# A new order of work and loads for the opening of a pooling and state-space decoder step, and a new order for the low parts of the pooled rows

## The chip, the cores and the metric

The kernel runs on one core of one Trainium2 chip. The metric is the device time of one execution in microseconds (us), lower is better. The core has a matrix engine (TensorE, PE in the profile), a vector engine (VectorE, DVE), a scalar engine (ScalarE, ACT), a general engine (GpSimd, POOL) and a sync engine (SP) that here only issues DMAs. Each engine runs its own queue of instructions strictly in order and waits for the others at semaphores.

## The reference

One layer of a hybrid decoder is computed for a prompt of 1024 rows and for 64 sample rows (8 sequences of 8), so 1088 rows in all. Cut to what matters:

```python
mod = silu(c) @ w_ada + b_ada
shift, scale, gate = split(mod, 3)
h = rmsnorm(x, norm_g) * (1 + scale) + shift
u_pool, z_pool, z_ssm, xbc, dt_raw, g_raw = split(h @ w_in, SPLITS)
p, pool_new = pool_mix(u_pool, pool_buf, pos0, pool_w, pool_scale)
p = (p * silu(z_pool)) @ w_pool_out
xbc_c, conv_new = causal_conv(xbc, conv_buf, conv_w, conv_b)
y, ssm_new = ssd(xs, dt, A, Bm, Cm, ssm_state)
s = rmsnorm((y + d_skip * xs) * silu(z_ssm), ssm_norm_g) @ w_ssm_out
m = sigmoid(g_pool) * p + sigmoid(g_ssm) * s
x = x + gate * (m @ w_o)
```

The width of the model is 1024, `w_in` has 8224 columns, and the pooling branch has four groups of 128 columns.

## The kernel before

**Stages.** First comes the opening (`first`): the rows of x are loaded, normalised and transposed, the modulation is multiplied out, and the first columns of `h @ w_in` are made. Then come the remaining columns of `h @ w_in` in pairs, by a Strassen scheme of 14 short products per pair (`strassen`, lines L412, L421, L426 and L434 in the profile). After them the chunks of the state-space scan run beside the products with `w_pool_out` and `w_ssm_out` (L227). The product with `w_o` ends the program.

**Two parts for every number.** Products run on a rounded type. So an operand is cut into a high part (a copy by ACT) and a low part (a subtraction, on DVE or POOL), and each product is made of three: high by high, low by high, high by low.

**The opening's order.** `ORDER1` is a list of some 350 words, written out by hand. Each word calls a small function that issues one or a few instructions; each engine then runs its own in that order (`in_line`). A letter at the end of a word sets the engine: V for DVE, A for ACT, G for POOL. The rows are treated in three blocks, 0 (rows 0 to 255), 1 (to 639) and 2 (to 1087); the 1024 columns in eight groups k of 128. The words that matter:

- `sq`, `root`, `unit`, `spread`, `rsb`: the norm of each row and its spreading over the partitions. `turn b.k` transposes a block on PE, `out b.k` takes it out of PSUM on DVE (L703, into a tile `tf`).
- `ada p.k`, `mr p`, `end p`, `md p`: part p (0 to 3) of the modulation, on PE, ACT, PE and DVE (L751, L754). Part p serves the columns k = 2p and 2p + 1.
- `h b.k` makes the high part of the modulated rows (ACT), `t` and `ta` the modulated rows themselves (L776 on ACT, L778 on DVE), `l b.k` their low part (a subtraction, L644). `hi`, `lo` cut weights in the same way, `wh`, `wl` those of the first Strassen pair.
- `pr b.k` are plain products of two weight columns (L817), `sg` takes them out through a sigmoid and stores them.
- `ca`, `cb`, `cc`, `ce` with k = 0 to 3 form the sums and differences of row halves in `tf` for the first Strassen pair (L644, 128x544); `s1` to `s4` cut these into high (`s1h`) and low parts (`s1l`). `ce3` is the last of the sums.
- `dR`, `dU`, `dL` are the products for the time steps (L843); they read the finished sums. `gt` are the products for the gate (L870), `ge` adds the gate's bias. `m i.s` are the 14 products of the first Strassen pair (L958), `u i.s` takes them out.
- `warm n` are n products of ones by ones with no use for the result (L726).

**The opening's loads.** They are issued by SP in the order of the list `waiting`; some have to wait for a word. SP has eight DMAs under way at most: each further one waits for the one eight before it. The loads of state rows for the first pooling and convolution units (L526, L528, L1068) are asked for later in the program, and the tile scheduler puts them where it finds room.

**The pooled rows.** `p_split` reads the four pooled groups back, makes their high parts on ACT and their low parts (L1575) on POOL for groups 0 and 2 and on DVE for 1 and 3. It is advanced step by step from `samples_beside`, which runs once after every product (seven a pair) in the last ten pairs; at the 70th call it issued all four low parts behind the last instruction of DVE. The first product of the next stage (L227) reads the low parts in the order 0, 1, 2, 3 as its last four terms.

Of the kernel before, what the change touches and what calls it, by code (L numbers as in the profile page):

```python
# [46 lines left out]
def tile_pool_ssd_step(  # L47
# [475 lines left out]
    def u_unit(gi):
        L = gi + 1
        stp = sm.tile([P, 120], F32, tag="stc", name=nm("stp"), bufs=4)
        load(stp, state_pool[gi])  # L526
# [14 lines left out]
        V.tensor_copy(us[:, :, 0:15], stv)  # L541
# [59 lines left out]
    ORDER1 = """
        warm20 sq0.A silu sq1.V turn0.3 turn0.5 turn0.2 tab vt sq2.V turn0.6 turn0.1 root0
        turn0.4 warm4 unit0.V sq3.A spread0 sq4.A warm2 rsb0.V out0.4 turn1.2 root1 turn1.5 warm5
        unit1.V out0.2 sq6.A out0.6 spread1 out0.3 out0.5 turn1.7 out0.1 rsb1.A turn1.3 sq7.V sq5.A turn1.6
        turn1.0 turn0.0 warm2 out1.5 sq8.A out1.2 turn2.5 out1.7 turn2.2 root2 out0.0 turn2.4 unit2.A out1.6
        turn2.7 out1.3 turn2.0 out1.0 turn2.1 spread2 ada0.0 rsb2.A ada0.2 out2.2 ada0.4 out2.7 ada0.6
        out2.1 mr0 turn2.3 out2.4 hi0.0 end0 out2.3 turn0.7 hi1.0 lo0.0.G turn1.4 md0 turn2.6 out0.7 turn1.1
        h1.0 out2.6 ada1.0 h0.0 lo1.0.V warm4 t0.0.A out1.4 h0.1 out2.0 ada1.2 t0.1.A l0.0.V warm1 ta2.0.A
        pr0.0 l0.1.V out2.5 t1.0.A pr0.1 t2.0 ta2.1.A out1.1 ada1.4 h2.0 l1.0.V ada1.6 h1.1 t2.1 l2.0.V
        pr1.0 mr1 h2.1 t1.1.A l2.1.G pr2.0 l1.1.V end1 pr2.1 md1 ta2.3.V h1.2 pr1.1 h0.3 t1.2.V t0.3.A t2.3  # L610
        ada2.0 l1.2.V h0.2 ada2.2 h2.3 t0.2.V ada2.4 hi0.1 l0.3.V l2.3.V ada2.6 h1.3 l0.2.V hi1.1 pr1.2
        t1.3.V mr2 lo1.1.V ta2.2.A end2 l1.3.G pr0.2 md2 pr0.3 t2.2 ta2.4.A lo0.1.V pr1.3 h1.4 t2.4 h0.5
        t1.4.V h2.2 ada3.0 t0.5.V h2.4 ada3.2 l2.2.V h1.5 ada3.4 l2.4.G h0.4 ada3.6 t1.5.A l0.5.V pr2.2 mr3
        dwd ta2.5.A l1.5.V t0.4.V end3 t2.5 pr2.3 l0.4.V h2.5 l1.4.G md3 pr0.4 h0.7 l2.5.V wh0 pr0.5 t0.7.V
        h0.6 wl0.V pr1.4 h1.6 tc.V h1.7 ca1.V m0.0 t0.6.A ca0.V s1h1 cb0.V s1h0 pr1.5 u0.0 cc0.V wh1 m0.1
        ce0.V ta2.7.A l0.6.V s4h0 wl1.V t1.6.A pr0.6 l0.7.V tb.V u0.1 pr2.4 wh4 d21.V t1.7.A l1.6.V pr0.7
        ta2.6.A wl4.V pr1.6 l1.7.V sgt t2.6 t2.7 m1.0 cb1.V sg0.0 cc1.V sg0.1 pr1.7 ce1.V h2.7 s1l0.V h2.6
        pr2.5 sg1.1 l2.7.V sg1.0 m1.1 l2.6.V d12.V s4h1 ca2.V pr2.6 wh5 cb2.V s1h2 ca3.V pr2.7 s1l2.V
        s1h3 cb3.V cc2.V gt0 wh3 u1.0 sg2.0 wl3.G u1.1 dR0 wh2 gt2 sg2.1 ce2.V dR1 cc3.V s2h0 gt4 wl2.V
        s4h2 dU1 ce3.V s2h3 s4l2.V s2h2 dL0 dUo1 s2l3.V dU0 s4h3 s2l0.V z1.0 s2l2.V gt6 dUo0 s1l3.V s2h1 dL1  # L620
        ge s4l1.G s3h0 dLo0 m2.0 s3h1 dLo1 s3h3 s3l1.V s3h2 s2l1.V m2.1 u2.0 dsL s3l3.V z1.1 s3l2.V m3.0
        s3l0.V wh6 u2.1 dRo1 wl6.G dRo0 m3.1 dsR u3.0 s4l3.V s1l1.V m4.0 nw u3.1 wl5.V m4.1 u4.0 s4l0.V m5.0
        n1 u4.1 nt3 m5.1 u5.0 nt2 z5.0 m6.0 u5.1 n2 m6.1 u6.0 z5.1 nd u6.1
    """.split()

    def first():
# [195 lines left out]
        def sg(b, t):  # L822
            o, n = BLK[b]
            if b < 2:
                buf = pa.tile([P, HF], F32, tag=("u3", "u2", "c2", "u3")[2 * b + t], name=nm("g0"))
# [4 lines left out]
            act(buf[:, :n], give(("pr", b, t))[:, :n], AF.Sigmoid)  # L830
# [169 lines left out]

        def bg_load():
            for j in range(4):
                load(bg[32 * j:32 * j + NB + 1], b_ada[0, 2 * D + 256 * j:2 * D + 256 * j + 256].partition_broadcast(NB + 1))
# [559 lines left out]
    def p_split():  # L1563
        ph, pl = Y4(hs), Y4(hs)
        ph_.extend(ph[:, gi] for gi in range(4))
        pl_.extend(pl[:, gi] for gi in range(4))
        for gi in range(4):
            load(pl[:, gi].bitcast(F32), yp_d[:, gi])
        yield
        for gi in range(4):  # L1570
            act(ph[:, gi], pl[:, gi].bitcast(F32), AF.Copy)
        yield
        for gi in range(4):
            y = pl[:, gi].bitcast(F32)
            (nc.gpsimd if gi % 2 == 0 else V).tensor_tensor(pl[:, gi], y, ph[:, gi].bitcast(F32), ALU.subtract)  # L1575
# [714 lines left out]
```

## Time and profile before

| | us |
|---|---|
| median of 3 runs | 1208.33 (1208.1 to 1209.11) |
| the profiled execution | 1206.63 |
| its span, first to last instruction | 1204.9 |
| DVE busy in the span | 915.8 |
| ACT busy | 661.4 |
| POOL busy | 815.0 |

In a row of a timeline the numbers are the start from the span's beginning and the time taken, both in us, then the engine, the line of the kernel, the operation, what it writes and reads, and the count. Square brackets give idle time of that engine just before, and who ended it. Neighbouring instructions on one engine overlap by some 0.05 to 0.1 us in these rows, since the next one starts while the last one is written out.

### The profile page before, as it was taken

How to read it: one execution, taken by the hardware profiler on the slowest of the kernel's cores; microseconds unless marked ns; L12 is line 12 of the kernel's file. 1: busy time of each engine (PE TensorE's matmuls, PEld its weight loads, DVE VectorE, ACT ScalarE, POOL GpSimd, SP SyncE). 2: the span in 40 equal slices, each digit the busy share in tenths (PEclk: the TensorE clock that was granted, in tenths of full speed). 3: DMA queues.
4: the chain of work that ended last, by engine and by line, in shares of the span. 5: the costliest groups of instructions: out<-in, count | busy, mean ns of one | idle time of the engine just before them, and what ended most of it. 6: DMA issues, size and time to landing. Idle time of an engine off the chain costs nothing.

```text
span 1204.9 us, 25116 instructions
## 1 busy us (share of the span) xinstructions
PE 1190.0 (99%) x9274; PEld 1125.3 (93%) x9274; DVE 915.8 (76%) x1567; ACT 661.4 (55%) x1511; POOL 815.0 (68%) x687
## 2 busy tenths in 40 slices
PE   9999999999999999999999999999999999999997
PEld 8879999999999999999999999999999989999885
DVE  6993689975979587877576564687888988679976
ACT  6864356475665556554534334566686766412435
POOL 1127878877988787755677776376889889523653
PEclk9999999999999999999999999999999999999999
DMA  9836445565546555454576767988788788595794
GB/s 352 305 133 208 141 137 180 185 212 149 185 157 201 172 160 164 149 166 137 191 241 239 239 220 252 322 311 267 238 273 297 263 293 282 204 337 157 236 208 158
DMA packets 156082, 262.69 MB, mean 218 GB/s; under 512 B 31280, under 2 KB 79160, under 8 KB 155960
## 3 DMA queue, kind: packets, MB, share of 16 engines
q1 hardware_dynamic: 87208, 171.25, 42.7%
q10 hardware_dynamic: 64592, 81.91, 19.7%
q0 software_dynamic: 4160, 7.94, 3.1%
q8 instruction: 73, 1.20, 0.4%
q14 instruction: 49, 0.40, 0.1%
HBM read 173.31 MB, written 87.73 MB: 217 GB/s over the span
## 4 chain that ended last, share of the span: by engine, by line
PE 82%; DVE 5%; DMA 4%; POOL 3%; ACT 3%; issue 2%; SPq 0%; DVEq 0%; POOLq 0%; ACTq 0%
PE mm L412 24%; PE ps L412 24%; PE mm L227 15%; PE pc L412 5%; PE ps L1246 2%; PE ps L1249 2%; DMA Y<-in_w_ada 1%; PE ps L2043 1%; PE ps L2042 1%; PE ps L2041 1%; DVE tf L644 1%; PE ps L1513 1%; PE ps L958 1%; PE pc L1335 1%; DMA G<-in_w_ada 1%
## 5 line engine op out<-in xcount | busy, mean ns | idle before, releaser
L227 PE MATMUL mm<-Y,w 128*128 128x352 f32 (+1 forms) x1440 | 255.4, 331 | 0.8 <-DVE G L1976 0.6
L227 PEld LDWEIGHTS mm<-Y,w 128*128 128x128 f32 x1440 | 235.3, 188 | 7.6 <-issue 4.6
L154 POOL TENSOR_TENSOR w<-rawA,w 128x512 fp32r<-128x512 f32 x120 | 181.7, 1518 | 78.6 <-ACT w L151 72.2
L154 POOL TENSOR_TENSOR w<-raw,w 128x512 fp32r<-128x512 f32 x90 | 157.2, 1753 | 62.9 <-ACT w L151 62.7
L412 PE MATMUL mm<-Y,w 128*128 128x272 f32 x1200 | 168.7, 289 | 0.0
L412 PE MATMUL ps<-Y,w 128*128 128x272 f32 x1200 | 167.8, 289 | 0.0
L412 PEld LDWEIGHTS mm<-Y,w 128*128 128x128 f32 x1200 | 156.8, 188 | 2.6 <-issue 1.0
L412 PEld LDWEIGHTS ps<-Y,w 128*128 128x128 f32 x1200 | 157.1, 188 | 0.8 <-issue 0.6
L151 ACT ACTIVATE w<-rawA 128x512 fp32r<-128x512 f32 x120 | 75.2, 626 | 95.1 <-PE ps L412 53.8
L1090 DVE SCALAR_TENSOR_TENSOR GA<-GA,cvT,GA 128x1112 f32<-128x1112 f32 x72 | 126.1, 1756 | 0.1
L151 ACT ACTIVATE w<-raw 128x512 fp32r<-128x512 f32 x90 | 56.0, 628 | 102.7 <-PE ps L412 33.7
L412 PE MATMUL mm<-G,w 128*128 128x272 f32 x720 | 101.2, 289 | 0.0
L412 PE MATMUL ps<-G,w 128*128 128x272 f32 x720 | 100.6, 289 | 0.0
L412 PEld LDWEIGHTS mm<-G,w 128*128 128x128 f32 x720 | 94.1, 188 | 1.2 <-issue 0.9
L412 PEld LDWEIGHTS ps<-G,w 128*128 128x128 f32 x720 | 94.4, 188 | 0.3 <-issue 0.3
L1234 ACT ACTIVATE dec<-dec,acT 128x128 f32<-128x128 f32 x256 | 78.6, 390 | 18.7 <-POOL dec L1230 18.6
L291 POOL TENSOR_TENSOR pw<-pw 128x512 fp32r<-128x512 f32 x40 | 65.6, 1639 | 11.5 <-ACT pw L290 11.5
L412 PE MATMUL pc<-Y,w 128*128 128x272 f32 x480 | 67.2, 288 | 0.0
L412 PEld LDWEIGHTS pc<-Y,w 128*128 128x128 f32 x480 | 62.6, 188 | 0.5 <-issue 0.4
L1470 POOL TENSOR_TENSOR Y<-xb,Y 128x512 fp32r<-128x512 f32 x32 | 41.5, 1296 | 25.0 <-ACT Y L1468 24.8
L1246 PE MATMUL ps<-dec,xd 128*64 128x128 f32 (+1 forms) x576 | 52.3, 273 | 0.6 <-DVE dec L1535 0.5
L1527 POOL TENSOR_TENSOR xl<-xw,xh 128x512 fp32r<-128x512 f32 x32 | 42.5, 1327 | 14.6 <-ACT xh L1526 14.6
(542 smaller groups left out, 2712.0 us busy)
## 6 DMA issues: line engine op xcount, KB each, us to landing
rawA<-in_w_in SPq DMA_DIRECT2D x62, 512.0 KB
ws<-pw ACTq DMA_DIRECT2D x32, 512.0 KB
dec<-acs_d SPq DMA_DIRECT2D x32, 512.0 KB
w<-ws SPq DMA_DIRECT2D x32, 512.0 KB
xbc<-GA ACTq DMA_DIRECT2D x24, 512.0 KB
wo<-ph SPq DMA_DIRECT2D x20, 512.0 KB
Y<-wo SPq DMA_DIRECT2D x10, 1024.0 KB
pw<-in_w_ssm_out ACTq DMA_DIRECT2D x32, 256.0 KB
```

What stands on the lines that cost most here:

```text
L151: ins = act(hi[:, :, :ncols], raw[:, :, :ncols], AF.Copy)
L154: (eng or nc.gpsimd).tensor_tensor(lo[:, :, :ncols], raw[:, :, :ncols], hi[:, :, :ncols].bitcast(F32), ALU.subtract)
L227: mm(ps[:, :n], w[k // 4][h][:, k % 4, :], r[k][:, o:o + n], start=(j == 0), stop=(j == len(terms) - 1))
L291: nc.gpsimd.tensor_tensor(raw.bitcast(F32R), raw, hi.bitcast(F32), ALU.subtract)
L412: mm(p, w[j // 8][:, k], A(k, s)[j // 4 == 1], start=(j == 0), stop=(j == 11))
L644: eng[e].tensor_tensor(dst, x, y, op)
L1090: V.scalar_tensor_tensor(d[:, :n], rp[:, k:k + n], cvT[:, 24 * k + mc:24 * k + mc + 1], d[:, :n], ALU.mult, ALU.add)
L1234: act(dec[:, h], dec[:, h], AF.Exp, bias=acT[:, c, 8 * g + h:8 * g + h + 1], scale=-1.0)
L1246: mm(o[hh], xd[:S, 2 * q + hh, :], dec[:S, 2 * q + hh], start=True, stop=state is None)
L1249: mm(o[hh], state[:, h * 64:h * 64 + 64], cE[:, h], start=False, stop=True)
L1470: nc.gpsimd.tensor_tensor(yl[g][:, :, o:o + S], v, yhc.bitcast(F32), ALU.subtract)
L1527: nc.gpsimd.tensor_tensor(xl, xw, xh.bitcast(F32), ALU.subtract)
```

## The change

The change has four parts: a new list `ORDER1`; a new order in `waiting`; the state loads of the first units put behind the load of the gate's bias; a new order of the low parts in `p_split`, now in two steps. One tag of a tile in `sg` changes too. Of `ORDER1` only the first line is shown; the diff below is cut to the rest.

```diff
     yp_ = [None] * 4
+    calm = []
...
-        load(stp, state_pool[gi])
         pwt = sm.tile([P, P], F32, tag="stc", name=nm("pwt"), bufs=4)
-        load(pwt, pool_w[0, gi])
+        with tc.issue_after(calm[0]):
+            load(stp, state_pool[gi])
+            load(pwt, pool_w[0, gi])
...
-        warm20 sq0.A silu sq1.V turn0.3 turn0.5 turn0.2 tab vt sq2.V turn0.6 turn0.1 root0
+        warm20 sq0.A silu sq1.V warm5 turn0.0 turn0.2 turn0.3 warm2 sq2.V tab root0 sq3.A sq4.A
...
-                buf = pa.tile([P, HF], F32, tag=("u3", "u2", "c2", "u3")[2 * b + t], name=nm("g0"))
+                buf = pa.tile([P, HF], F32, tag=("u3", "u2", "c2", "g3")[2 * b + t], name=nm("g0"))
...
         def bg_load():
             for j in range(4):
-                load(bg[32 * j:32 * j + NB + 1], b_ada[0, 2 * D + 256 * j:2 * D + 256 * j + 256].partition_broadcast(NB + 1))
+                ins = load(bg[32 * j:32 * j + NB + 1], b_ada[0, 2 * D + 256 * j:2 * D + 256 * j + 256].partition_broadcast(NB + 1))
+            calm.append(ins.ins)
...
-        for what in ("x01", "vb", "x27", "smp", "p0", "w", "p1", "p2"):
+        for what in ("x01", "x24", "vb", "x57", "w0", "smp", "p0", "w1", "p1", "p2"):
...
-            elif what == "w":
-                waiting += [((), lambda t=t: w_load(t, 0)) for t in range(2)]
+            elif what[0] == "w":
+                waiting += [((), lambda t=int(what[1]): w_load(t, 0))]
...
         stc = sm.tile([P, 24], F32, tag="stc", name=nm("stc"), bufs=4)
-        load(stc, state_conv[mc])
+        with tc.issue_after(calm[0]):
+            load(stc, state_conv[mc])
...
-        for gi in range(4):
+        for gi in (0, 2, 1, 3):
             y = pl[:, gi].bitcast(F32)
             (nc.gpsimd if gi % 2 == 0 else V).tensor_tensor(pl[:, gi], y, ph[:, gi].bitcast(F32), ALU.subtract)
-        yield
+            if gi % 2:
+                yield
...
-        if due[0] == 7 * LAST:
+        if due[0] in (7 * LAST - 1, 7 * LAST):
             with behind(mybir.EngineType.DVE):
                 next(p_in)
```

In the new `ORDER1` thirteen words have another engine. From POOL to DVE go `lo0.0`, `l2.1`, `l1.3`, `l2.4`, `l1.4`, `wl3` and `s4l1`; from ACT to DVE `ta2.1` and `t0.3`; from DVE to ACT `unit1`, `t0.2` and `t0.4`; from DVE to POOL `l0.5`. The `warm` words fall from seven to six (38 products to 36). Beyond the opening and the low parts, the engines' sequences stay as they were.

POOL in the opening, before; a name is the tile written, then the tiles read, and the first row is a memset at the program's start:

```order
21 L999 MEMSET bg 128x256
22 L644 TENSOR_TENSOR w_489<-raw_243,w_489 128x512
23 L644 TENSOR_TENSOR Y_520<-tf_310,Y_519 128x448
24 L644 TENSOR_TENSOR Y_520<-tf_290,Y_519 128x384
25 L644 TENSOR_TENSOR G_761<-tf_315,G_760 128x448
26 L644 TENSOR_TENSOR G_761<-tf_315,G_760 128x384
27 L644 TENSOR_TENSOR w_1057<-raw_931,w_1057 128x512
28 L644 TENSOR_TENSOR Y_520<-tf_294,Y_519 128x544
29 L644 TENSOR_TENSOR w_1213<-rawA_715,w_1213 128x512
```

And now (L649 is L644 of before):

```order
21 L1004 MEMSET bg 128x256
22 L649 TENSOR_TENSOR G_747<-tf_363,G_746 128x256
23 L649 TENSOR_TENSOR w_1207<-rawA_709,w_1207 128x512
24 L154 TENSOR_TENSOR w_1249<-rawA_1245,w_1249 128x512
25 L154 TENSOR_TENSOR w_1305<-rawA_1245,w_1305 128x512
```

The seven subtractions `lo0.0`, `l2.1`, `l1.3`, `l2.4`, `l1.4`, `wl3` and `s4l1` have left POOL, and `l0.5` (row 22) has come; the weight of the last product, `wl6`, stays.

SP, whose rows are DMAs, in the middle of the opening, before:

```order
17 L798 DMA raw_263<-in_w_in 128x512
18 L526 DMA stp_1366<-in_state_pool 128x120
19 L528 DMA pwt_1368<-in_pool_w 128x128
20 L1068 DMA stc_1640<-in_state_conv 128x24
21 L1068 DMA stc_1642<-in_state_conv 128x24
22 L798 DMA raw_500<-in_w_in 128x512
23 L197 DMA G_595<-in_w_ada 128x1024
```

And now (L803 is L798 of before):

```order
17 L803 DMA raw_263<-in_w_in 128x512
18 L803 DMA raw_505<-in_w_in 128x512
19 L197 DMA G_594<-in_w_ada 128x1024
20 L197 DMA G_596<-in_w_ada 128x1024
21 L197 DMA G_598<-in_w_ada 128x1024
22 L197 DMA G_600<-in_w_ada 128x1024
23 L509 DMA dtw<-in_w_dt 128x256
```

The four state loads are gone from between the second halves of the plain products' weights; they now stand behind the four loads of the gate's bias.

DVE around the last of the sums (`ce3`, row 122 before, which makes `tf_366`), before:

```order
119 L644 TENSOR_TENSOR tf_306<-tf_306,tf_298 128x544
120 L644 TENSOR_TENSOR tf_290<-tf_366,tf_290 128x544
121 L644 TENSOR_TENSOR w_1071<-rawA_633,w_1071 128x512
122 L644 TENSOR_TENSOR tf_366<-tf_366,tf_290 128x544
123 L644 TENSOR_TENSOR Y_520<-tf_306,Y_519 128x544
124 L644 TENSOR_TENSOR Y_1090<-tf_290,Y_1090 128x544
125 L644 TENSOR_TENSOR Y_1090<-tf_385,Y_1090 128x544
126 L644 TENSOR_TENSOR Y_1090<-tf_298,Y_1090 128x544
```

And now (`ce3` is row 123, L981 is L976 of before):

```order
121 L649 TENSOR_TENSOR tf_303<-tf_358,tf_303 128x544
122 L981 TENSOR_TENSOR c_127_1086<-s_109_895,ps_994 128x272
123 L649 TENSOR_TENSOR tf_358<-tf_358,tf_303 128x544
124 L981 TENSOR_TENSOR c_127_1086<-s_109_895,ps_962 128x272
125 L649 TENSOR_TENSOR Y_1082<-tf_295,Y_1082 128x544
126 L649 TENSOR_TENSOR Y_1082<-tf_303,Y_1082 128x544
127 L649 TENSOR_TENSOR Y_1082<-tf_299,Y_1082 128x544
128 L649 TENSOR_TENSOR w_1063<-rawA_622,w_1063 128x512
129 L649 TENSOR_TENSOR S_1061<-tf_358,S_1061 128x544
130 L649 TENSOR_TENSOR Y_521<-tf_349,Y_520 128x544
131 L649 TENSOR_TENSOR w_1133<-raw_906,w_1133 128x512
```

One `u1` (row 124), the weight `wl2` (row 128) and the weight `wl3` from POOL (row 131) now stand behind `ce3` on DVE.

More of the change, by code (lines that the diff above doesn't have):

```diff
@@ L601, in tile_pool_ssd_step @@
     ORDER1 = """
-        warm20 sq0.A silu sq1.V turn0.3 turn0.5 turn0.2 tab vt sq2.V turn0.6 turn0.1 root0
[L603 to L621, printed above, removed]
@@ L622, in tile_pool_ssd_step @@
-        s3l0.V wh6 u2.1 dRo1 wl6.G dRo0 m3.1 dsR u3.0 s4l3.V s1l1.V m4.0 nw u3.1 wl5.V m4.1 u4.0 s4l0.V m5.0
-        n1 u4.1 nt3 m5.1 u5.0 nt2 z5.0 m6.0 u5.1 n2 m6.1 u6.0 z5.1 nd u6.1
+        warm20 sq0.A silu sq1.V warm5 turn0.0 turn0.2 turn0.3 warm2 sq2.V tab root0 sq3.A sq4.A
+        unit0.V vt spread0 rsb0.V turn0.4 out0.4 root1 turn1.2 out0.2 warm4 unit1.A turn0.1 turn0.6 out0.6
+        spread1 turn1.7 turn1.5 out0.3 sq6.A turn0.5 rsb1.A turn1.3 out1.5 turn1.0 out0.5 sq7.V out1.0 sq5.A
@@ new lines, in tile_pool_ssd_step @@
+        sq8.A out0.1 out1.7 root2 turn2.0 turn1.6 turn0.7 out1.3 unit2.A out0.7 turn1.1 out1.2 turn1.4 turn2.5
+        out1.4 out0.0 spread2 rsb2.A turn2.1 turn2.2 hi0.0 turn2.7 ada0.0 ada0.2 out2.1 ada0.4 out2.5 ada0.6
+        out1.1 warm4 out2.2 mr0 out1.6 end0 turn2.4 lo0.0.V out2.0 md0 turn2.3 hi1.0 out2.7 out2.4
+        h0.0 h0.1 lo1.0.V turn2.6 ada1.0 ada1.2 t0.0.A l0.0.V t0.1.A ta2.0.A pr0.0 h1.0 t2.0 l0.1.V
+        t1.0.A h2.0 warm1 pr0.1 out2.3 t2.1 out2.6 l1.0.V ada1.4 ada1.6 mr1 h1.1 ta2.1.V t1.1.A
@@ new lines, in tile_pool_ssd_step @@
+        l2.0.V pr1.0 l1.1.V h2.1 end1 pr2.0 md1 pr1.1 ta2.3.V l2.1.V pr2.1 ada2.0 h0.3 h1.2
+        ada2.2 h0.2 t0.3.V t2.3 ada2.4 h2.3 t0.2.A t1.2.V l1.2.V l2.3.V ada2.6 h1.3 hi1.1 pr1.2
+        l0.2.V l0.3.V t1.3.V mr2 end2 ta2.2.A lo1.1.V t2.2 pr0.2 md2 hi0.1 ta2.4.A t2.4 h0.5
+        l1.3.V pr0.3 lo0.1.V pr1.3 ada3.0 h1.4 t0.5.V ada3.2 h2.2 h1.5 h2.4 t1.4.V ada3.4 l2.2.V
+        h0.4 ada3.6 pr2.2 mr3 dwd t0.4.A l0.5.G t1.5.A end3 pr2.3 l0.4.V wh0 md3 h0.7
+        ta2.5.A t2.5 l1.4.V h1.7 h2.5 h0.6 l2.4.V h1.6 l1.5.V pr2.4 wl0.V pr0.4 tc.V t0.7.V
@@ L624, in tile_pool_ssd_step @@
+        s2l0.V s2h2 dL0 z1.0 s2h1 s2l3.V s2l2.V dL1 dUo1 wh3 wl2.V dUo0 s1l3.V s4l2.V
+        gt6 s3h0 wl3.V dLo1 s3h3 s4h3 m2.1 s3h1 dLo0 s2l1.V m2.0 s3l0.V s3h2 ge
+        z1.1 s3l1.V u2.0 m3.0 wh6 wl6.G s3l2.V u2.1 s3l3.V m3.1 dRo1 dRo0 u3.1 u3.0
+        s1l1.V m4.0 nw m4.1 dsR s4l1.V wl5.V u4.0 s4l0.V s4l3.V m5.0 nt3 m5.1 dsL
+        u5.0 u4.1 n1 nt2 m6.0 u5.1 n2 u6.0 z5.0 m6.1 z5.1 nd u6.1
     """.split()
```

6 lines of the change are left out of this document (added).

## The prediction

> **What bounds the kernel now.** The page first, then the windows of 25.9 to 72.4 us:
>
> ```profile
> PE 1190.0 (99%) x9274; PEld 1125.3 (93%) x9274; DVE 915.8 (76%) x1567; ACT 661.4 (55%) x1511; POOL 815.0 (68%) x687
> ```
>
> ```profile
> core 0: us, PE busy (x) PEld busy (x) DVE busy (x) ACT busy (x) POOL busy (x), PEclk, DMA share, GB/s
> 25.90:72.40 46.50, 44.39 (x479) 37.33 (x467) 43.49 (x92) 37.83 (x71) 8.17 (x6) 1.00 0.68 256
> ```
>
> PE is busy 99% of the span, so only a stage in which PE waits, or runs below its pace, can give time back. The opening is one: it ends when the first Strassen product behind it starts, and from there PE runs dense for hundreds of us in an unchanged order. So the change is worth what it moves that start. The window shows who paces it: DVE is busy 43.49 of 46.50 us, more than ACT, and PE's timeline names DVE at its last stop:
>
> ```profile
> 72.49 0.87 PE L843 MATMUL ps<-tf,dtw 128*32 128x272 f32 x9 [0.57 <-DVE tf L644]
> ...
> 90.43 1.68 PE L412 MATMUL ps<-Y,w 128*128 128x272 f32 x12
> ```
>
> The time-step products (L843) wait for the sums on DVE; `ce3` frees the last. Behind them stand fourteen products of 1.5 us, four of them done early, and the stage ends at 90.43.
>
> **Part 1: DVE between `md0` and `ce3`.** DVE's and POOL's timelines side by side:
>
> ```profile
> 24.46 1.29 POOL L644 TENSOR_TENSOR w<-raw,w 128x512 fp32r<-128x512 f32 x1 [19.88 <-ACT w L802]
> ...
> 38.94 1.53 POOL L644 TENSOR_TENSOR Y<-tf,Y 128x384 fp32r<-128x384 f32 x1 [5.35 <-PE mm L817]
> 43.44 2.30 POOL L644 TENSOR_TENSOR G<-tf,G 128x448 fp32r<-128x448 f32 x2 [2.97 <-ACT G L769]
> 66.80 1.38 POOL L644 TENSOR_TENSOR w<-raw,w 128x512 fp32r<-128x512 f32 x1 [21.06 <-ACT w L802]
> 68.14 1.84 POOL L644 TENSOR_TENSOR Y<-tf,Y 128x544 fp32r<-128x544 f32 x1
> ```
>
> ```profile
> 25.11 0.67 DVE L754 TENSOR_TENSOR md<-md,vT 128x18 f32<-128x18 f32 x1
> 25.70 0.17 DVE L751 TENSOR_TENSOR md<-ps,vT 128x18 f32<-128x18 f32 x1
> ...
> 34.12 0.18 DVE L754 TENSOR_TENSOR md<-md,vT 128x18 f32<-128x18 f32 x1
> ...
> 39.71 0.80 DVE L754 TENSOR_TENSOR md<-md,vT 128x18 f32<-128x18 f32 x1
> ...
> 43.47 1.40 DVE L644 TENSOR_TENSOR G<-tf,G 128x256 fp32r<-128x256 f32 x1
> 44.79 1.09 DVE L644 TENSOR_TENSOR dwd<-dtw 128x128 f32<-128x128 f32 x1
> ...
> 46.99 0.42 DVE L644 TENSOR_TENSOR G<-tf,G 128x256 fp32r<-128x256 f32 x1
> ...
> 66.96 1.80 DVE L644 TENSOR_TENSOR tf<-tf,tf 128x544 f32<-128x544 f32 x1
> ...
> 69.38 1.82 DVE L644 TENSOR_TENSOR tf<-tf,tf 128x544 f32<-128x544 f32 x2
> ...
> 71.72 0.71 DVE L644 TENSOR_TENSOR tf<-tf,tf 128x544 f32<-128x544 f32 x1
> ```
>
> The same DVE instruction takes 0.18 us alone and 0.67 or 0.80 beside POOL, 0.42 alone and 1.40 beside POOL, 0.71 and 1.80. So a subtraction given to POOL isn't free for DVE. Summed between `md0` (ends 25.87) and `ce3` (ends 72.43): 0.62 at 39.71, 0.98 at 43.47, 0.8 at 44.79 (half of 0.42 as the undisturbed time, its row being half as wide), 1.09 at 66.96 and 0.4 at 69.38 (1.82 less twice 0.71), together **3.9 us**. The order rows show that all six POOL subtractions of this stretch (the window's x6) leave POOL and that only one short one, `l0.5`, comes. A pair as wide cost DVE 1.78 in 2.30 us of POOL; for 256 columns in place of 832 I take 0.6. Contention falls by **3.3 us**.
>
> What does DVE take on? Groups by line and shape in that window:
>
> ```profile
> L644 DVE TENSOR_TENSOR w<-raw,w 128x512 fp32r<-128x512 f32 x4 | 2.7, 684 | 0.0
> ...
> L778 DVE TENSOR_SCALAR tf<-tf,md 128x384 f32<-128x384 f32 x4 | 1.9, 479 | 0.3 <-ACT Y L767 0.3
> ...
> L703 DVE TENSOR_TENSOR tf<-mm,rsb 128x448 f32<-128x448 f32 x3 | 1.8, 610 | 0.0
> ...
> L644 DVE TENSOR_TENSOR G<-tf,G 128x448 fp32r<-128x448 f32 x3 | 1.8, 622 | 0.0
> ...
> L644 DVE TENSOR_TENSOR G<-tf,G 128x384 fp32r<-128x384 f32 x3 | 1.6, 549 | 0.0
> L778 DVE TENSOR_SCALAR tf<-tf,md 128x256 f32<-128x256 f32 x4 | 1.6, 411 | 0.4 <-ACT Y L767 0.3
> ```
>
> New between the two marks: `l2.1` and `l2.4` (0.62 each), `l1.3` and `l1.4` (0.55 each), `ta2.1` and `t0.3` (0.48 each), three `out` of block 2 (0.61 each): 5.13. Gone from it: `t0.2`, `t0.4` and `out0.7` (0.41 each), `l0.5` (0.42), `out1.1` and `out1.4` (taken as `l` of 384, 0.55 each), two `out` of block 2 (1.22), one `u1` (taken as 0.42), `wl2` (0.68): 5.07. That is **no change** in work; what counts is that POOL's part is gone.
>
> Waits: DVE stood idle 46.50 less 43.49, 3.0 us. The longest named:
>
> ```profile
> DVE Y L644 <- ACT tf L776: 1.1, 2, 0.9
> DVE tf L778 <- ACT Y L767: 0.5, 2, 0.3
> DVE R L644 <- ACT R L909: 0.4, 1, 0.4
> ```
>
> ```profile
> ACT g L830 <- DMA gs<-g: 1.0, 1, 1.0
> ```
>
> The last is ACT waiting for a store to free the tile that `sg` uses twice; the new tag takes it away, and ACT feeds DVE. Going through both queues with these durations, ACT mostly has its tile ready now. Nothing in the rows excludes that the waits stay (0) or go (-3.0); I take the middle, **-1.5 us**.
>
> The Trainium skill has a rule for the contention, in SBUF — State Buffer, section "Who interferes with whom": a DVE instruction with two SBUF inputs and a GpSimd instruction that reads SBUF exclude each other for the whole instruction. The trace agrees in kind, though 3.9 us were lost beside 7.05 us of POOL in these rows; by full blocking the sum below would be some 3 us lower, an estimate from that page, whose case stands among the rivals.
>
> **Part 2: the loads.** SP's and ACT's timelines:
>
> ```profile
> 15.46 8.35 SPq L197 DMA_DIRECT2D G<-in_w_ada  x8
> 24.76 0.33 SPq L798 DMA_DIRECT2D raw<-in_w_in  x1
> ...
> 31.20 0.33 SPq L798 DMA_DIRECT2D raw<-in_w_in  x1
> 32.46 2.79 SPq L197 DMA_DIRECT2D G<-in_w_ada  x4
> ```
>
> ```profile
> 17.34 1.06 ACT L659 ACTIVATE sqj<-R 64x1024 f32<-64x1024 f32 x1 [1.30 <-DMA R<-in_x_sample]
> ```
>
> Eight loads of 512 KB leave in 8 us, so a load of 256 KB is about 0.6 us of the queue. The new order puts one (`w0`) ahead of the sample rows, on which ACT waits at 17.34 and behind it the norm of block 2: **+0.6**. Behind that norm DVE had five `out` of 448 ahead of `md0`; now it has four, two of 384 and `lo0.0`: 2.44 + 1.10 + 0.68 less 3.05, some +1.0 once the overlap of rows is taken off. In return `md0` no longer stands beside POOL (0.67 against 0.18, -0.5). So `md0` ends **1.1 us later**. Nothing hides it: DVE is full from there on.
>
> The four state loads between 24.76 and 31.20 held up the last plain weight by about 5 us and the loads of part 3 by as much. These also wait for PE to have read the tiles that they overwrite, so only a part of that is gained, and DVE's list asks for neither much earlier than before; I count nothing here beyond the -1.5 of waits. What covers the state loads in their new place:
>
> ```profile
> 50.28 4.12 SPq L1003 DMA_DIRECT2D bg<-in_b_ada  x4
> ```
>
> ```profile
> 87.17 0.21 DVE L541 COPY us<-stp 128x120 f32<-128x120 f32 x1
> ```
>
> The bias is issued by 54.4 and the first pooling unit reads its state at 87, so some 30 us of other work hide them.
>
> **Part 3: behind `ce3`.** One `u1`, `wl2`, `wl3` and `s4l1` now stand behind `ce3` on DVE (0.42 + 0.68 + 0.68 + 0.71, 2.5 us). From `ce3` to 90.43 there are 18.0 us, and PE is bound by its own products; the fourth pair of them needs the low parts of the second sums. PE reaches it some 6 us after `ce3`, DVE has them after 6 to 7. Bounds: 0 (the order covers it) and +2.5 (all of it shows). I take **+0.5**, near the lower end.
>
> **Part 4: the low parts of the pooled rows.** DVE's and PE's timelines there:
>
> ```profile
> 757.53 2.49 DVE L1575 TENSOR_TENSOR Y<-Y,Y 128x1088 fp32r<-128x1088 f32 x2
> ```
>
> ```profile
> 757.66 2.15 PE L227 MATMUL mm<-Y,w 128*128 128x384 f32 x11
> 760.07 6.37 PE L227 MATMUL mm<-Y,w 128*128 128x384 f32 x37 [0.25 <-DVE Y L1575]
> ```
>
> PE runs eleven terms at 0.17 each (6.37 by 37), to 759.55, and then the twelfth waits for DVE's second low part: 0.5 us. A step earlier, the first one falls into DVE's idle time before 757 and the second ends by about 759: **-0.5**. What DVE does behind them isn't needed by PE before 766.
>
> **Sum.** -3.3 + 0 - 1.5 + 1.1 + 0.5 - 0.5 = -3.7 us. On the profiled execution: span 1204.9 to 1201.2, and with 1.7 us around it 1206.6 to 1202.9. The median of the runs, 1208.33, lies 1.7 above that execution, so I forecast **1204.6 us**. A measurement of this kernel can tell about 0.2% (2.4 us) from no change.
>
> **Rivals.**
>
> *The tail takes it back.* The 2.5 us behind `ce3` show in full, because `wl6`, still on POOL, blocks DVE there too, and PE then waits at the second sums and the sums after them. Then -3.7 - 0.5 + 2.5 = -1.7, or less where the waits of part 1 stay: about 1207. For it: DVE is busy 43.5 of 46.5 us before `ce3` and has more behind it now. Against: PE needs 12 us for its last eight products, and DVE's list is worked off within them.
>
> *DVE simply has more to do (slower).* Nine words went to DVE (5.4 us) and four left (1.9). If the long rows are not POOL's doing, but come from waits that the rows don't show, they stay, and the opening ends 3.5 us later; with +0.6 of the sample's load and -0.5 of part 4 that is 1211.9. It decides from the point where DVE rows of over 1 us stand without POOL beside them. Against: each of the long rows lies within or just behind a POOL row.
>
> *Full blocking.* POOL costs DVE its whole time, hidden in part as idle time, and most waits go: -3 further, 1201.6. The rows of 43 to 46 (1.78 lost beside 2.30) speak for it, that of 69.38 (0.4 beside 1.84) against.
>
> *The change does less than it says.* The loads come sooner to no purpose and ACT, with 37.8 of 46.5 us, becomes the pace instead of DVE: half of part 1, about 1206.7.
>
> **Chances and range.** Forecast 0.52 (its own range 1203 to 1206.3), tail 0.18, ACT as the pace 0.12, full blocking 0.10, slower 0.08. Faster by over 0.2% means below 1205.9: most of the forecast's 0.52 (0.48), full blocking 0.10, and 0.04 of the tail and ACT cases, so **0.62**. Within 0.2%: **0.30**. Slower: **0.08**. The range takes in full blocking and the tail with the bound of its cost: 1201.5 to 1208.8.
>
> **What would show each step.** Right: POOL busy under 2 us between `md0` and `ce3`, the 128x256 rows of DVE near 0.42; `md0` near 27, `ce3` near 69, the first L412 product near 87.2; no wait for a low part in the first L227 product. Wrong: `ce3` near 69 but L412 near 89 (tail); long DVE rows without POOL (more to do); DVE idle well over 3 us, waiting for ACT (ACT as the pace); `md0` later than 28, by which the loads would cost more than the 0.6 counted.

## The result, and the profile after

| | before | after |
|---|---|---|
| median of 5 runs (of before: the three above and two more), us | 1208.33 (1207.87 to 1209.8) | 1202.6 (1201.35 to 1202.64) |
| the profiled execution | 1206.63 | 1201.66 |
| its span | 1204.92 | 1199.92 |

The ratio is 0.9947, with a 95% interval of 0.9933 to 0.996: faster by about 0.5%. The forecast was 1204.6, the range 1201.5 to 1208.8. Between the two medians lie 5.7 us and between the two profiled spans 5.0, where the sum of the prediction had 3.7.

Engine shares of the page of after, and the window between the end of `md0` (25.9) and that of `ce3` (67.7), as busy time and count of each engine:

```profile
PE 1187.6 (99%) x9270; PEld 1125.2 (94%) x9270; DVE 917.3 (76%) x1570; ACT 662.9 (55%) x1514; POOL 807.3 (67%) x681
```

```profile
core 0: us, PE busy (x) PEld busy (x) DVE busy (x) ACT busy (x) POOL busy (x), PEclk, DMA share, GB/s
25.90:67.70 41.80, 41.80 (x473) 37.22 (x475) 39.10 (x92) 36.38 (x68) 0.97 (x1) 1.00 0.72 273
```

The page's first line hardly moves; the window does. It is 41.8 us long in place of 46.5, POOL is down from 8.17 to 0.97, DVE from 43.49 to 39.10, and PE, with 44.39 of 46.50 before, is now busy in all of it. The marks of the prediction, in us from the start of the span:

| | before | after | lead of after |
|---|---|---|---|
| `md0` ends | 25.87 | 25.93 | -0.06 |
| `ce3` ends | 72.44 | 67.72 | 4.72 |
| first L412 product | 90.43 | 86.06 | 4.37 |
| first L227 product | 757.66 | 753.29 | 4.37 |
| thirteenth L227 product | 760.35 | 755.45 | 4.90 |
| span | 1204.92 | 1199.92 | 5.00 |

Between L412 and L227, over 660 us, the lead stays 4.37 to the second decimal: the dense stretch carries on what the opening gained. The first row hides something: in five other executions of the new order with the new list of loads `md0` ends at 24.88 to 25.19, some 0.7 to 1.0 us sooner than here; the experiments on the loads show why. DVE and PE of after at the places that the prediction showed:

```profile
41.44 1.09 DVE L649 TENSOR_TENSOR Y<-tf,Y 128x448 fp32r<-128x448 f32 x1
42.45 0.28 DVE L649 TENSOR_TENSOR dwd<-dtw 128x128 f32<-128x128 f32 x1
...
67.00 0.72 DVE L649 TENSOR_TENSOR tf<-tf,tf 128x544 f32<-128x544 f32 x1
...
750.16 1.28 DVE L1582 TENSOR_TENSOR Y<-Y,Y 128x1088 fp32r<-128x1088 f32 x1
...
753.15 1.28 DVE L1582 TENSOR_TENSOR Y<-Y,Y 128x1088 fp32r<-128x1088 f32 x1
```

```profile
41.07 0.97 POOL L649 TENSOR_TENSOR G<-tf,G 128x256 fp32r<-128x256 f32 x1 [36.50 <-DVE tf L783]
77.11 1.31 POOL L649 TENSOR_TENSOR w<-rawA,w 128x512 fp32r<-128x512 f32 x1 [35.07 <-ACT w L807]
```

```profile
28.45 0.38 PE L731 MATMUL ps<-ones 128*128 128x128 f32 x2
...
86.06 1.68 PE L412 MATMUL ps<-Y,w 128*128 128x272 f32 x12
...
753.29 8.25 PE L227 MATMUL mm<-Y,w 128*128 128x384 f32 x48
```

The one long DVE row of the stretch, 1.09 us at 41.44, stands beside the one POOL row left; `dwd` is 0.28 in place of 1.09, the last sum of 544 columns 0.72 in place of up to 1.80. The two low parts of the pooled rows now stand three us apart, and the first four L227 products, of twelve terms each (x48), run without a stop. (Lines of after are 5 to 7 higher than those of before: the fillers' L726 is L731.)

### The profile page after: what moved, and what is told of

It is laid out like the page before. It is cut to its first block, busy times and chain, and to the rows that moved or that the text cites. A ratio compares the mean times of both kernels' runs of the same rounds, so it can differ in the third digit from the quotient of the medians.

```text
span 1199.9 us, 25096 instructions
## 1 busy us (share of the span) xinstructions
PE 1187.6 (99%) x9270; PEld 1125.2 (94%) x9270; DVE 917.3 (76%) x1570; ACT 662.9 (55%) x1514; POOL 807.3 (67%) x681
## 4 chain that ended last, share of the span: by engine, by line
PE 85%; POOL 5%; DMA 3%; DVE 3%; issue 2%; ACT 1%; SPq 0%; POOLq 0%; ACTq 0%; DVEq 0%
PE mm L412 24%; PE ps L412 24%; PE mm L227 11%; PE pc L412 5%; PE ps L1253 2%; PE ps L2051 2%; PE ps L2049 2%; PE ps L2050 2%; PE ps L963 1%; DMA R<-in_w_o 1%; PE ps L822 1%; PE ps L1256 1%; PE mm L822 1%; POOL Y L1477 1%; PE pc L731 1%
## 5 line engine op out<-in xcount | busy, mean ns | idle before, releaser
L227 PE MATMUL mm<-Y,w 128*128 128x352 f32 (+1 forms) x1440 | 255.1, 331 | 0.6 <-DVE G L1984 0.6
L227 PEld LDWEIGHTS mm<-Y,w 128*128 128x128 f32 x1440 | 235.4, 188 | 7.0 <-issue 4.8
L412 PE MATMUL mm<-Y,w 128*128 128x272 f32 x1200 | 168.7, 289 | 0.0
L412 PE MATMUL ps<-Y,w 128*128 128x272 f32 x1200 | 167.8, 289 | 0.0
L412 PEld LDWEIGHTS mm<-Y,w 128*128 128x128 f32 x1200 | 156.8, 188 | 2.6 <-ACT w L151 0.8
L412 PEld LDWEIGHTS ps<-Y,w 128*128 128x128 f32 x1200 | 157.1, 188 | 0.8 <-issue 0.6
L151 ACT ACTIVATE w<-raw 128x512 fp32r<-128x512 f32 x90 | 56.2, 629 | 110.5 <-DVE raw L349 41.8
L412 PE MATMUL mm<-G,w 128*128 128x272 f32 x720 | 101.2, 289 | 0.0
L412 PE MATMUL ps<-G,w 128*128 128x272 f32 x720 | 100.6, 289 | 0.0
L412 PEld LDWEIGHTS mm<-G,w 128*128 128x128 f32 x720 | 94.1, 188 | 1.2 <-issue 0.9
L412 PEld LDWEIGHTS ps<-G,w 128*128 128x128 f32 x720 | 94.4, 188 | 0.3 <-issue 0.3
L412 PE MATMUL pc<-Y,w 128*128 128x272 f32 x480 | 67.2, 288 | 0.0
L412 PEld LDWEIGHTS pc<-Y,w 128*128 128x128 f32 x480 | 62.6, 188 | 0.5 <-issue 0.4
```

What stands on the lines that cost most here:

```text
L151: ins = act(hi[:, :, :ncols], raw[:, :, :ncols], AF.Copy)
L227: mm(ps[:, :n], w[k // 4][h][:, k % 4, :], r[k][:, o:o + n], start=(j == 0), stop=(j == len(terms) - 1))
L412: mm(p, w[j // 8][:, k], A(k, s)[j // 4 == 1], start=(j == 0), stop=(j == 11))
```

## The experiments

Executions of the same code differ by up to 1 us before `md0`, and kernels alike behind L227 by up to 4 us there (438.9 to 443.2 from the first L227 product to the last matmul), so the medians tell a few of the differences only; **stretches inside one trace** tell more. Kernels with the same opening agree in them: before, before_again and lows_alone took 64.56 to 65.06 us from `md0` to the first L412 product, after, old_lows and old_wait_list 60.13 to 60.19. before_again, the same code as before, moved by 0.5 us at `ce3` and L412, more than the 0.3 that had been expected of it; so a difference of over 0.5 us in such a stretch is taken as real, and a smaller one is not read.

| kernel | median (runs), us | ratio to before | `md0` to `ce3` | `md0` to L412 | `md0` to L227 |
|---|---|---|---|---|---|
| before | | | 46.57 | 64.56 | 731.79 |
| after | 1202.6 (5) | 0.9933 to 0.996 | 41.79 | 60.13 | 727.36 |
| before_again | 1210.23 (1) | | 47.06 | 65.06 | 732.29 |
| old_lows | 1202.28 (4) | 0.9924 to 0.9954 | 41.83 | 60.19 | 727.41 |
| lows_alone | 1207.84 (11) | 0.9977 to 0.9997 | 46.91 | 64.88 | 732.11 |
| pool_back | 1203.76 (8) | 0.9944 to 0.9972 | 41.98 | 61.47 | 728.69 |
| pool_off | 1205.44 (6) | 0.9955 to 0.9989 | 44.64 | 62.73 | 729.83 |
| old_wait_list | 1203.57 (6) | 0.9942 to 0.9974 | 41.81 | 60.17 | 727.40 |
| states_early | 1202.51 (4) | 0.9931 to 0.9962 | 43.05 | 61.33 | 728.56 |
| states_held_alone | 1208.05 (10) | 0.9987 to 1.0012 | 46.82 | 64.79 | 732.02 |
| off_and_held | 1206.93 (10) | 0.998 to 0.9998 | 45.19 | 63.28 | 730.38 |
| fill_after | 1204.73 (6) | 0.996 to 0.9983 | 43.13 | 61.42 | 728.65 |
| fill_before | 1208.79 (10) | 0.9995 to 1.0015 | 46.12 | 64.09 | 731.32 |
| lean_no_pool | 1204.86 (9) | 0.9964 to 0.9983 | 41.56 | 62.94 | 730.16 |

The median of before was 1209.28 in the first set (pool_back, pool_off, old_lows, lows_alone), 1208.44 in the second (before_again, states_early, old_wait_list, states_held_alone) and 1208.5 in the third.

### Pooled rows: old_lows, lows_alone

old_lows is after with the old low parts, lows_alone is before with the new:

```diff
-        for gi in range(4):
+        for gi in (0, 2, 1, 3):
...
+            if gi % 2:
+                yield
...
-        if due[0] == 7 * LAST:
+        if due[0] in (7 * LAST - 1, 7 * LAST):
```

> The changed kernel with the low parts of the pooled rows as before (order 0, 1, 2, 3, one step at the 70th call). Theory: the opening stays (first L412 product at 86.06) and PE stands 0.5 us before the twelfth term of the first L227 product, the lead of 4.9 us behind it falls to 4.4; 0.5 us in all. Rival (the lows are hidden): no wait and no difference at that place.

> The kernel before with only the new order of the low parts, two steps. Theory: the opening stays (first L412 product at 90.43), the 0.5 us wait before the twelfth term of the first L227 product goes, and the span is 0.3 to 0.5 us shorter. Rival: the place of the wait moves to another term and nothing is gained.

PE's timeline of old_lows:

```profile
752.60 2.15 PE L227 MATMUL mm<-Y,w 128*128 128x384 f32 x11
755.01 6.38 PE L227 MATMUL mm<-Y,w 128*128 128x384 f32 x37 [0.25 <-DVE Y L1582]
```

The stop ahead of the twelfth term is back. From term eleven to twelve it takes 0.59 us in before and old_lows, 0.17 in after and lows_alone: the step is worth 0.42 us, in both orders. In the whole time neither run can show it: old_lows has a median of 1202.28 against 1202.6 of after.

### POOL's words: pool_back, pool_off

pool_back is after with seven words on POOL again and `l0.5` on DVE; pool_off is before with the opposite edit:

```diff
-lo0.0.G l2.1.G l1.3.G l2.4.G l1.4.G wl3.G s4l1.G l0.5.V
+lo0.0.V l2.1.V l1.3.V l2.4.V l1.4.V wl3.V s4l1.V l0.5.G
```

> The kernel before, with nothing changed but the engine of eight words: the seven subtractions of POOL go to DVE, l0.5 from DVE to POOL. Theory (contention): DVE loses its long rows, ce3 ends 2 to 3.5 us before 72.4, the first L412 product starts 1.5 to 3.5 us before 90.43. Rival (DVE is the engine with the most to do, so more words on it cost their own time): seven words of 0.55 to 0.7 us more, one of 0.4 less, ce3 ends 1 to 2 us later (the two behind it apart), L412 2 to 4 us later.

> The changed kernel, but the seven subtractions lo0.0, l2.1, l1.3, l2.4, l1.4, wl3 and s4l1 are POOL's again and l0.5 is DVE's. Theory (POOL beside DVE costs DVE time, more than the subtraction itself would): the long DVE rows come back (over 1 us for 128x256 or 128x544), about 3.3 us between md0 and ce3 less nothing gained, ce3 moves from 67.7 to about 70 to 71, the first L412 product from 86.06 to 88 to 89.5, and the time rises by 2 to 3.5 us. Rival (the order of the words and the loads made the gain, DVE only has fewer words now): DVE has some 4 us less work of its own, ce3 stays at 67.7 or comes sooner, and the time stays within 1 us.

In the old order the engines alone give 1.9 to 2.4 us up to `ce3` and 2.0 to 2.5 to L227 (against before and before_again), about half of the change. The excess of DVE's rows over the undisturbed row of the same shape, summed between `md0` and `ce3`, is 4.4 us in before beside 8.25 of POOL, 0.5 in after beside 0.97, and 0.5 in pool_off beside 1.12 of its one POOL row, `l0.5`. So pool_off went as its theory had it.

In the new order it is another thing. DVE's and POOL's timelines of pool_back:

```profile
31.95 1.03 DVE L759 TENSOR_TENSOR md<-md,vT 128x18 f32<-128x18 f32 x1
...
42.08 1.11 DVE L649 TENSOR_TENSOR dwd<-dtw 128x128 f32<-128x128 f32 x1
```

```profile
31.78 1.16 POOL L649 TENSOR_TENSOR Y<-tf,Y 128x448 fp32r<-128x448 f32 x1 [9.27 <-ACT Y L774]
...
82.10 1.78 POOL L649 TENSOR_TENSOR Y<-tf,Y 128x544 fp32r<-128x544 f32 x1
```

The contention is back (3.4 us of excess beside 5.25 of POOL), and yet `ce3` ends 41.98 us behind `md0`, as in after (41.79), not the 3.3 us later that the theory had. DVE itself is busy for 1.1 us more (40.18 against 39.10), since four subtractions of the stretch left it and `l0.5` came. What is lost, 1.2 us, is lost behind `ce3`, where PE waits for POOL's own low part:

```profile
83.93 1.14 PE L963 MATMUL mm<-Y,w 128*128 128x272 f32 x7 [1.21 <-POOL Y L649]
```

So DVE's time doesn't seem to set the end of `ce3` any more; something else does. That asked for the fillers below.

### Loads: old_wait_list, states_early, states_held_alone, off_and_held

old_wait_list is after with the opening's list of loads of before; states_early is after with the state loads free to go early; states_held_alone is before with them held; off_and_held is before with them held and with pool_off's edit. (before_again is the kernel before, unchanged.)

```diff
-        for what in ("x01", "x24", "vb", "x57", "w0", "smp", "p0", "w1", "p1", "p2"):
+        for what in ("x01", "vb", "x27", "smp", "p0", "w", "p1", "p2"):
```

```diff
-        with tc.issue_after(calm[0]):
-            load(stc, state_conv[mc])
+        load(stc, state_conv[mc])
```

> The changed kernel with the old list of loads (vecs behind the first two rows tiles, both first plain weights behind part 0); the state loads stay behind the bias. What I first took (256 KB ahead of the sample rows cost 0.6 us): the sample's norm and md0 come 0.6 us sooner than 25.9. Rival (the list of loads is why md0 did not come later: vecs behind five tiles lets the rows land sooner): the sample lands at 17.3 as before, rsb of block 2 ends at 22.2 or later instead of 21.6, md0 ends at 26.4 to 27, and L412 starts 0.3 to 1 us later than 86.06.

> The kernel before, unchanged, as a measure of how much the marks of the opening move from one execution to another: md0 at 25.9, ce3 at 72.4 and the first L412 product at 90.4, each within 0.3 us. Where they move by more, differences between single profiles of below that are not read.

Every mark of old_wait_list lies within 0.05 us of after, `md0` at 25.88 against 25.93. But the list does something all the same; the two executions are late for different reasons. With the new list ACT begins the squares of the sample rows at 16.02 to 16.49 us (six executions), with the old one at 16.90 to 17.91 (eight, old_wait_list among them), although the new list issues their load later (7.25 us in after, 5.94 in old_wait_list). ACT's rows in after and in states_early, both with the new list, and in old_wait_list:

```profile
16.25 1.06 ACT L664 ACTIVATE sqj<-R 64x1024 f32<-64x1024 f32 x1
```

```profile
16.15 1.06 ACT L663 ACTIVATE sqj<-R 64x1024 f32<-64x1024 f32 x1 [1.01 <-DMA R<-in_x_sample]
```

```profile
17.28 1.06 ACT L664 ACTIVATE sqj<-R 64x1024 f32<-64x1024 f32 x1 [1.67 <-DMA R<-in_x_sample]
```

In old_wait_list ACT waits for the load until 17.28. In after it comes to the rows a us later than in states_early and finds them landed. PE's first row shows why, in after and then in fill_after (a run of below), whose code is the same up to `md0`:

```profile
1.07 8.69 PE L731 MATMUL pc<-ones 128*128 128x128 f32 x50 [1.07 <-POOL ones L117]
```

```profile
1.07 7.65 PE L731 MATMUL pc<-ones 128*128 128x128 f32 x50 [1.07 <-POOL ones L117]
```

These are the 25 fillers ahead of the first transposes (two records each). Their records start 0.21 us apart at first and 0.11 us apart from some moment on: from 6.99 us in after, from 4.64 to 5.50 us in the six other executions of the new order. So the first transposes start at 9.59 us in after and at 8.47 to 8.85 in the others, and DVE and ACT, which need them, are late too: DVE waits 1.19 us for PE at 11.34 in after, 0.16 at 10.31 in fill_after. In the five others with the new list `md0` ends at 24.88 to 25.19, in old_wait_list, with quick fillers, at 25.88. By this one execution the list is worth 0.7 to 1.0 us ahead of `md0`, as the rival had it in kind (the 0.6 us sooner that I first took did not come), and the profile of after, with its slow fillers, does not show it. Why the sample rows land sooner with the new list was not tried.

> The changed kernel without the wait of the state loads: they stand between the plain weights again, four places ahead of the last plain weight and of part 3 of the modulation. Theory (the loads of part 3 wait for their tiles anyway and DVE asks for nothing sooner): md0, ce3 and L412 move by less than 0.5 us (L412 at 86 to 86.6). Rival (the sooner loads feed a part of the opening that was waiting): hi1.1, md2 or md3 come 1 to 3 us later and L412 starts at 87 to 89.

> The kernel before with only the state loads behind the bias. Theory: ce3 and L412 stay within 0.5 us of 72.4 and 90.4. Rival: the last plain weight, ready 5 us sooner, and part 3, ready some 2 us sooner, shorten the waits of ACT and DVE and L412 starts 1 to 2 us sooner.

With the state loads early, SP issues part 3's loads 4.9 us later (32.22 against 27.36), and PE comes to part 3 before they have landed. SP and PE of states_early, then SP and PE of after:

```profile
32.22 2.76 SPq L197 DMA_DIRECT2D G<-in_w_ada  x4
...
41.24 0.64 PE L740 MATMUL pc<-G,scT 128*32 128x128 f32 x16 [0.16 <-DMA G<-in_w_ada]
42.55 0.64 PE L740 MATMUL pc<-G,scT 128*32 128x128 f32 x16 [0.67 <-DMA G<-in_w_ada]
```

```profile
27.36 3.78 SPq L197 DMA_DIRECT2D G<-in_w_ada  x4
...
40.97 1.96 PE L741 MATMUL pc<-G,scT 128*32 128x128 f32 x64
```

In the new order holding them is worth 1.2 us from `md0` on (728.56 less 727.36), as the rival had it. The theory's mark, L412 at 86 to 86.6, is met (86.26) only because `md0` comes 1.0 us sooner than in after, with quicker fillers; and the median, 1202.51 against 1202.6, does not show the loss. In the old order holding them is worth nothing (732.02 against 731.79 and 732.29).

> The kernel before, its order of words unchanged, with the seven POOL words on DVE and l0.5 on POOL, and with the state loads held behind the gate's bias. Alone the first gave L227 less md0 of 729.83 (from 732.05), the second nothing (732.02). Additive: 729.8. If the loads begin to count once DVE has room (in the new order they were worth 1.2): 728.6. The new order has 727.4, so 1.2 to 2.4 us stay as the worth of the order of the words by itself.

It is worth nothing there even when DVE has been relieved: 730.38, if anything later than the 729.83 of pool_off. From L227 of after to that of these two kernels it is still 2.5 to 3.0 us, of 4.4 to 4.9 in all: these need the rest of the change, that is the order of the words, the places of the fillers, the five other letters (`unit1`, `ta2.1`, `t0.2`, `t0.3`, `t0.4`) and the tag of `sg`.

### Who paces the opening: fill_after, fill_before

Six fillers more on PE, in each order, at the same two words. Nobody reads them.

```diff
                 pm[p] = PC() if p else beat[0]
+                if p > 1:
+                    for _ in range(3):
+                        mm(pm[p][:, 256:256 + P], ones, ones, start=True, stop=True)
```

> The changed kernel with six more filler products of 128 columns on PE, three ahead of the first AdaLN product of part 2 and three ahead of that of part 3; nobody reads them, and no other engine gets more work. A filler leaves two records of some 0.12 us (8 records 1.16 us in the rows of before), so PE gets about 1.4 us. Theory (in the new order PE is the pace of the opening): md0 to the first L412 product goes from 60.13 to 61.2 to 61.6, and L227 less md0 from 727.4 to 728.5 to 728.8. Rival (DVE still paces, as the prediction had it for the old order): PE's fillers fall into its waits, 60.1 to 60.5. Second rival (ACT paces): as the first.

> The kernel before with the same six fillers at the same two words. In its stretch from md0 to the first L412 product (64.56) PE has some 5 us of stops beyond its pace. Theory (DVE is the pace of the old order, PE that of the new): the fillers are taken out of those stops, 64.6 to 65.0, L227 less md0 within 0.5 of 732.05. Rival (PE's products, in their order, were the pace of both, and the old order only adds stops at other places): +1.1 to +1.5 here too, 65.7 to 66.1.

The stretches between `md0` and `ce3` of fill_after and fill_before, in the columns of the window above:

```profile
25.00:68.10 43.10, 43.10 (x485) 38.83 (x486) 39.06 (x91) 36.46 (x68) 0.73 (x1) 1.00 0.71 274
```

```profile
26.70:72.80 46.10, 44.81 (x491) 40.10 (x483) 43.42 (x92) 37.76 (x71) 8.61 (x6) 1.00 0.69 259
```

PE's timelines, the first lot of fillers in each:

```profile
34.25 0.83 PE L741 MATMUL pc<-ones 128*128 128x128 f32 x6
```

```profile
36.40 0.83 PE L736 MATMUL pc<-ones 128*128 128x128 f32 x6
```

The same 0.83 us of PE, twice in each kernel. In the new order they lengthen the way to L412 by 1.29 us (60.13 to 61.42) and the way to L227 by 1.29 too; in the old one not at all (64.09, against 64.56 to 65.06; why it is even 0.5 to 1.0 us shorter isn't shown). At these two places PE paces the new opening, and did not pace the old. The medians go the same way (1204.73 against 1202.6, and 1208.79 against 1208.5), though kernels with the opening of after have medians of 1202.28 to 1203.57 themselves.

### A leaner order: lean_no_pool

After without the five fillers behind the second norm, and with the last two POOL words on DVE:

```diff
-out1.1 warm4 out2.2
+out1.1 out2.2
...
-h2.0 warm1 pr0.1
+h2.0 pr0.1
...
-l0.5.G wl6.G
+l0.5.V wl6.V
```

> The changed kernel, with the five fillers behind the second norm left out (four ahead of the first mean row, one behind h2.0) and with l0.5 and wl6 on DVE in place of POOL. Theory (PE is the pace): md0 to the first L412 product loses only the one filler in it, 0.2 to 0.3 (59.8 to 60.0), and nothing for l0.5 and wl6, though DVE has about 0.9 us less of contention; up to 0.5 before md0; in all 0.2 to 0.8 us, less than the runs can tell. Rival (DVE paces): 0.5 to 0.9 from the contention, 59.2 to 59.6.

Up to `ce3` the theory held: 0.23 us for the one filler behind `md0`, and nothing for a DVE with 0.5 us less of contention. Behind `ce3` it lost 3.0 us (21.38 from `ce3` to L412, against 18.34), which neither case had. DVE's and PE's timelines of lean_no_pool there:

```profile
76.32 0.69 DVE L649 TENSOR_TENSOR w<-rawA,w 128x512 fp32r<-128x512 f32 x1 [1.19 <-ACT w L807]
```

```profile
77.70 0.39 PE L963 MATMUL ps<-Y,w 128*128 128x272 f32 x1 [0.72 <-DVE Y L649]
78.33 2.40 PE L963 MATMUL ps<-Y,w 128*128 128x272 f32 x17 [0.25 <-DVE Y L649]
...
82.69 0.65 PE L963 MATMUL mm<-R,w 128*128 128x272 f32 x3 [0.95 <-DVE w L649]
```

`wl6` on DVE waits 1.19 us for ACT's high part, and the low parts queued behind it come late for PE, whose stops in these rows are 1.9 us of the 3.0. The same word on POOL, at 77.11 in after, held up nobody. None of these kernels is clearly faster than after; old_lows and states_early can't be told from it by their medians.

## Why the prediction was right, and where it wasn't

**What held.** The place (the opening, and one stop at L227), the sign, and the contention of POOL as a cost of the old order, which pool_off shows. From `md0` to `ce3` the forecast was -3.3 of contention and -1.5 of waits, in all -4.8; measured -4.78. That these agree so closely is luck, as the next paragraphs show. Behind `ce3` +0.5; measured +0.35 (17.99 to 18.34). Pooled rows -0.5; measured -0.42 from the stop itself, -0.53 in the lead.

**The term that failed: `md0` 1.1 us later.** In the profile of after it ends 0.06 us later than before, in five other executions with the new order and list 0.7 to 1.0 us sooner. Its part on DVE was right in kind: from the end of the spreading of block 2's norm to `md0` it takes 4.33 us, before 3.66, so +0.67 where 0.5 was counted (+1.0 less 0.5). The part of the load, +0.6 for `w0` ahead of the sample rows, had the wrong sign. A wait of 1.30 us at one ACT row was priced by the time that one more load takes in the queue; but with the new list, where the sample rows are issued later, ACT begins their squares 1.1 us sooner (16.25 against 17.34). This term holds most of the miss. An estimate: `md0` 0.7 to 1.0 sooner, the 4.43 us of the stretch up to L412 and the 0.53 at L227 make 5.6 to 6.0 us, beside 5.7 between the medians and a forecast of 3.7. The medians alone can't prove that sum, since executions differ by several us behind L227.

**Right sum, wrong split.** DVE's busy time in the stretch fell by 4.4 us (43.49 to 39.10), its idle time only from 3.01 to 2.70. The excess of rows fell by 3.9 (4.4 to 0.5; forecast 3.3, which left out the row of 1.01 us at 32.99) and the work itself by 0.5 (forecast 0). Of the waits, -1.5 by the forecast, only 0.3 went; the waits view of DVE in after still has two long ones, behind ACT:

```profile
DVE G L649 <- ACT tf L781: 1.1, 1, 1.1
DVE Y L649 <- ACT tf L781: 0.7, 1, 0.7
```

**Why the gain has the size it has.** The prediction took DVE as the bound on both sides. PE was not the bound before, where six fillers cost nothing, and relieving DVE alone (pool_off) paid. It is the bound after: the same six cost 1.29, and giving DVE its contention back (pool_back) costs nothing clear up to `ce3`. So the gain ends where PE runs out of stops. PE's stops beyond its pace between `md0` and the first L412 product, summed over the matmul starts that lie more than 0.26 us apart (less 0.15 for each), are 5.0 us in before and 1.6 in after, 3.4 less (4.1 or 3.3 less with 0.20 or 0.30 in place of 0.26); in fill_before they are 3.2, which is where its fillers went. And four of the five fillers behind `md0` (the 1.65 us of rows at 26.10 and 27.76 in before, one row of 0.38 in after) now stand ahead of it, at 0.21 each (1.29 by six) another 0.86; ahead of `md0` they cost less, since the way from the norm to `md0` is only 0.16 shorter in lean_no_pool, which leaves them out. Together 4.3 of the 4.43 us that the stretch lost. That a filler which cost nothing before would cost its full time afterwards was not in the prediction.

**The loads of part 3, counted at nothing.** Right for the old order, wrong for the new. In the new order PE reaches part 3 some 13.6 us behind the issue of its loads at 27.36; issued at 32.22, they are late.

**The rivals.** *The tail* didn't take it back, but its place was right: pool_back and lean_no_pool, which put `wl3` and `s4l1`, and `wl6`, on the other engine, lost 1.2 and 3.0 us there. Which engine makes a low part decides in that stage, not how much DVE has to do before it. *More to do on DVE* fell with pool_off: the long rows go when POOL's words go. *ACT as the pace* is not what the runs show: with 36.38 of 41.80 us busy it is not far off, but PE's fillers add in full. *Full blocking*, with the rule of the Trainium skill in SBUF — State Buffer, section "Who interferes with whom" (a DVE instruction with two SBUF inputs and a GpSimd one exclude each other for the whole instruction): in the rows of this case that is so, one row at a time. Between `md0` and `ce3` there are 40 such long two-input rows of DVE in twelve executions; each began inside a POOL subtraction and ended 0.13 to 0.14 us before the sum of POOL's end and the row's own undisturbed time. In before POOL's row of 66.80 ends at 68.18, and DVE's of 66.96, 0.71 alone, at 68.76; in after POOL's ends at 42.04, and DVE's of 41.44, 0.62 alone, at 42.53. Each POOL subtraction lengthens one such row, by what is left of POOL's when DVE's starts, 0.4 to 1.2 us. So the excess is only half to two thirds of POOL's time (4.4 beside 8.25 in before, 0.47 beside 0.97 in after, 3.4 beside 5.25 in pool_back), and the rival's further 3 us did not show: DVE's idle time fell by 0.3. The row of 69.38, which the prediction took as a sign against it, fits as well: it began 0.60 us before POOL's end. One more row, a TENSOR_SCALAR of fill_after at 40.71, began 0.10 us before POOL's and was lengthened all the same, from 0.48 to 1.04 us.

**What stays open.** The new tag of the tile that `sg` uses twice was not run by itself; ACT's wait of 1.0 us for a store is no longer among its waits in after. Why the new order has fewer PE stops is shown only for the state loads and POOL's words; the remaining 2.5 to 3.0 us belong to the rest of the change as a whole, and no single move in it was tried. PE was tested as the pace at two places of the opening, and no run gave ACT more to do. The worth of the new list rests on one execution of the old one, in the new order, and what makes the sample rows land sooner is open.

## What to carry to other kernels

Before an engine is relieved, find out how much slack the next one has: a few dead instructions on it, which cost nothing now and their full time afterwards, show when the bound has moved. Fillers and helpers that were free while one engine paced have to be counted again once another does; the 25 fillers ahead of the first transposes are such a case, and their time differed by a us between two executions of the same code. And an edit that is worth nothing alone (the state loads) can be worth a us behind another one, so parts of a change are tested in both orders, taken out of the new and put into the old.

## What the runs showed of the hardware

What a DVE subtraction lost to POOL went by where it began inside POOL's instruction, not by its size: 128x18 took 1.03 us at 31.95 in pool_back, 0.18 alone in before. Rows that read PSUM were not lengthened: the two of L976 at 68.69 and 69.03 in before, inside the POOL row of 68.14, took 0.43 each.

Products of ones by ones at the program's start stood 0.21 us apart per record up to a moment between 4.00 and 6.99 us, and 0.11 us from there on; the moment differed between executions of the same code (6.35 in before, 4.00 in before_again). Marks behind it are compared by their distances, not by their times.
